# Input projection of a hybrid encoder layer: product sums kept on PSUM copies, two of four weight sums made by accumulating DMAs

## The chip, the cores and the metric

The kernel runs on one core of one Trainium2 chip. The metric is the device time of one execution in microseconds (us). Before the change it is 901.23 us, the median of three runs (899.83 to 901.51).

## The reference

One layer of an encoder is applied to 768 tokens of width 1024 (a batch of 512 and a batch of 256 tokens, side by side), in float32:

```
x    = layernorm(x_in)
proj = x @ w_in                                   # 1024 -> 3072: bg, cg, hc, q, k, v
y    = concat(rmsnorm(bg * dwconv3(cg * hc)), rmsnorm(neighbourhood_attention(q, k, v)))
x    = layernorm(ALPHA * x + y @ w_o)
u    = dwconv3(x @ w_up); gate, val = split(u)
out  = layernorm(ALPHA * x + (gelu(gate) * val) @ w_down)
```

The part that changes is `x @ w_in` without the v columns (2560 of the 3072 columns), and what reads its results.

## The kernel before

Every float32 operand of a matrix product is split into a rounded high part and the remainder (`split`, line 100: a ScalarE copy, then a subtraction on VectorE or GpSimd). A product is three matmuls of parts for each of four blocks of 128 rows, so twelve matmuls.

The input projection and the up projection multiply 2 x 2 blocks with seven products in place of eight (a Strassen-Winograd scheme). The operands on the token side are seven sums of quarters of x, kept as `AR[:, o]`; on the weight side there are seven sums of quarters of two weight blocks (g and v: q with k, cg with hc, or two bg blocks). One such set is a *pair*. The input projection has ten pairs (`SEQB`, line 342), so 70 products or 840 matmuls (line 185). Each product covers 384 token columns.

A pair before (`Pair`, line 153; `pair_steps`, line 517):
- **weights**: four quarters are loaded by SyncE's queue (SP, line 123) into a ring of six raw buffers (`NRAW`). GpSimd (POOL) makes the four weight sums as 128x512 additions (line 162). Each of the seven weight operands is then split into a ring of six `w4` buffers (ScalarE line 101, VectorE line 102).
- **products**: in the order 1, 6, 2, 5, 7, 3, 4. The products 1 and 2 share one PSUM bank, 7 and 4 share another, the other three have one each: five banks' worth a pair, taken from four `r` banks.
- **sums of products**: product 1 is copied to SBUF by ScalarE (line 531); VectorE then makes five 128x384 additions a pair out of PSUM (lines 533, 538, and three in `c22`, `c12`, `c21` of the classes `QK`, `CH`, `BB`), each of which also adds an SBUF tile.

The weights of pair n+1 are split product by product while pair n is multiplied. Between the products stand attention steps (S products, softmax, transposes, O products: `att_steps`, line 584; how many after which product is written by hand in `RATE`), and GpSimd also builds the attention's bias (line 566), issues its DMAs and adds squares (line 430). The order on SP is the program's. The other engines' order in this stage is made by a compile-time scheduler that goes by program order as priority and estimated times; each engine then runs its list in order.

Ahead of this stage come the layer norm of x, its transposes, the v projection (line 308) and the seven token operands (`x_t_sums`); the first pair's weights are split there too (`SEQA`, line 365, an order by hand, with `P7` as its last entry). After it come the output projection (lines 765, 787), the up projection (line 863, its own class `Pair` at line 838) and the down projection (line 1015).

The up projection does its pairs differently, and the change brings its way to the input projection. It loads five buffers a pair, two of which get the other quarter added by an accumulating DMA that GpSimd issues (lines 846, 847); VectorE makes the other two weight sums (lines 853, 856). The products run in the order 1, 7, 6, 2, 4, 5, 3. ScalarE copies product 1's bank to a second PSUM bank (line 917), product 6 is accumulated on the copy, that is copied again (line 924), and products 2, 4, 5 and 3 are accumulated on those three banks; product 7 is copied to SBUF (line 921) and added twice by VectorE (lines 932, 936).

Of the kernel before, what the change touches and what calls it, by code (L numbers as in the profile page):

```python
# [34 lines left out]
NRAW, NW4, NST = 6, 6, 2  # L35
NWD, NHO, NUP = 10, 10, 11
# [11 lines left out]
def encoder_kernel(ctx, tc, x, lnp, wv, wproj, wo_a, wo_c, wup, wdn, chan, rpb, mask, ident, out):  # L48
# [22 lines left out]
    def big(name):  # L71
        return ps.tile([P, 1024], F32, name=name, tag="big", bufs=2)

# [29 lines left out]

    SE = G
# [46 lines left out]
    late = {}  # L151

    class Pair:


        def __init__(self, a11, a12, a21, a22):
            self.a = {1: a11, 2: a12, 21: a21, 4: a22}
            self.t, self.o = {}, {}

        def tmp(self, i, x, y, sub, dst=None):  # L160
            t = self.t[i] = late["s"].tile([P, 512], F32, name="stmp", bufs=NST) if dst is None else dst
            (SE.tensor_sub if sub else SE.tensor_add)(t, x, y)
            return t

        def sums(self, d5=None, d6=None):
            a = self.a
            self.tmp(5, a[21], a[4], False, d5)
            self.tmp(6, self.t[5], a[1], True, d6)
            self.tmp(7, a[1], a[21], True, a[21])

        def get(self, i, tag="w4", eng=V):
            a = self.a
            if i in (5, 6) and 5 not in self.t:
                self.sums()
            if i == 3:
                self.tmp(3, a[2], self.t[6], True, a[2])
            src = a[i] if i in (1, 2, 4) else self.t[i]
            self.o[i] = wsplit(src, eng=eng) if tag == "w4" else wsplit(src, late["s"], "w4b", 2, eng)
            return self

    def prod(pi, i, q, start=True, stop=True, ks=range(4), n=slice(0, 384)):
        w = pi.o[i].rearrange("p h (k n) -> p h k n", k=4)
        for k in ks:
            for m, (g, h) in enumerate(((0, 0), (0, 1), (1, 0))):
                PE.matmul(q[:, n], w[:, g, k], ar(OPS[i])[:, h, k, n], start=start and k == 0 and m == 0,  # L185
                          stop=stop and k == 3 and m == 2, skip_group_check=i in (1, 2, 4, 7))
# [156 lines left out]
    for z in SEQB:  # L343
        p = int(z[2])
        g, v = (wproj[c * 4 + m] for c, m in {"qk": ((3, p), (4, p)), "ch": ((1, p), (2, p)), "bb": ((0, p), (0, p + 1))}[z[:2]])
        stm.add(Pair, g[:, 0:512], g[:, 512:1024], v[:, 0:512], v[:, 512:1024])
    stm.load(1)
# [9 lines left out]
    late["s"] = a1  # L357
    ORDER = (1, 6, 2, 5, 7, 3, 4)
    stm.ahead = 1
    pb = [stm.next(0)]  # L360
    stm.ahead = 2
    PW = engs("VGVGVVG")
    TA = (0, 2, 1, 3, 4, 5)
    EA = {"L": lambda i: ln_in(TA[i]), "x": lambda i: x_t(TA[i]), "v": lambda i: v_proj(TA[i], 0), "u": lambda i: v_proj(TA[i], 1), "T": x_t_sums, "P": lambda o: pb[0].get(o, eng=PW[ORDER.index(o)]), "w": lambda k: wv_prep(k, k + 1), "l": stm.load}
# [10 lines left out]
    late["s"] = a2  # L375
# [10 lines left out]
    y_d = dram.tile([2, 4, P, T], F32, name="y_d")  # L386

# [14 lines left out]
    def k_split(src, u):  # L402
        for n, m in ((slice(256 * u, 256 * u + 256), slice(0, 256)), (slice(NS + P * u, NS + P * u + P), slice(256, 384))):
            A.activation(kh[:, n], src[:, m], AF.Copy, scale=0.125)
            V.scalar_tensor_tensor(kl[:, n], src[:, m], 0.125, f(kh[:, n]), op0=OP.mult, op1=OP.subtract)
# [14 lines left out]
    def y_parts(hi, lo, src, i):  # L420
        A.activation(hi, src, AF.Copy, scale=gng[:, i:i + 1])
        V.scalar_tensor_tensor(lo, src, gng[:, i:i + 1], f(hi), op0=OP.mult, op1=OP.subtract)
# [16 lines left out]
    cy, by = {}, {}  # L439

    class QK:
# [3 lines left out]
        def c11(self, q):  # L445
            q_split(q, 0)

        def c22(self, q, t):
            z = stt()
            V.tensor_add(z, q, t)  # L450
            k_split(z, 1)

        def c12(self, q, t):
            V.tensor_add(t, q, t)
            q_split(t, 1)

        def c21(self, q, s):
            V.tensor_add(s, q, s)
            k_split(s, 0)

    class CH:
        def __init__(self, p):
            self.p = p
            self.c = a2.tile([P, T], F32, name="cp", tag="c3", bufs=2)
            self.x = a2.tile([P, T], F32, name="cc", tag="c3", bufs=2)

        def mul(self, z, u):
            for n, m, w in ((256 * u, 0, 256), (NS + P * u, 256, P)):
                V.tensor_mul(self.x[:, n:n + w], z[:, m:m + w], self.c[:, 384 * u + m:384 * u + m + w])

        def c11(self, q):
            A.copy(self.c[:, 0:384], q)

        def c22(self, q, t):
            self.z = stt()
# [232 lines left out]
    for _ in att:  # L708
        pass
# [448 lines left out]
```

## Time and profile before

| What | Value |
|---|---|
| median of three runs | 901.23 us |
| the profiled execution, whole time | 901.13 us |
| its span in the profile | 898.8 us |
| before the input projection | 0 to 61.6 us |
| input projection with attention | 61.6 to 275.0 us |
| output projection, norm, token operands | 275 to 400 us |
| up projection | 400 to 704 us |
| down projection and last norm | 704 to 898.8 us |

TensorE is busy 94% of the span, VectorE 75%, ScalarE 50%, GpSimd 27%. In the tables PE is TensorE's matmul, PEld its weight load, DVE is VectorE, ACT ScalarE, POOL GpSimd, SPq the DMA queue of SyncE. PEclk is the granted TensorE clock as a share of full speed. A row of grouped instructions gives the line, engine, operation, output<-inputs and count, then the busy time and mean duration (ns) of one, then the idle time of the engine just before them with what ended it.

### The profile page before, as it was taken

The page shows a single profiled execution, that of the slowest core. Times are in us where ns is not written, and L with a number is a line of the kernel's source. Part 1 is how long each engine was busy: PE and PEld are TensorE (multiplying, and loading weights), DVE is VectorE, ACT ScalarE, POOL GpSimd, SP SyncE. Part 2 cuts the span into 40 slices and gives each one's busy share as a digit, 9 for nine tenths or more (in the row PEclk, how much of TensorE's full clock was granted, in tenths as well). Part 3 has the DMA queues.
Part 4 walks back from the last instruction along what each step waited for, and adds up shares of the span by engine and source line. Part 5 has one row for each costly group of instructions (what it writes and reads, how often), then busy time and mean ns, then how long its engine had stood idle before and what let it go on. Part 6 is the DMA issues. An engine that isn't in the chain of part 4 may idle for free.

```text
span 898.8 us, 12782 instructions
## 1 busy us (share of the span) xinstructions
PE 840.7 (94%) x4425; PEld 777.3 (86%) x4425; DVE 671.4 (75%) x1204; ACT 447.9 (50%) x893; POOL 242.4 (27%) x269
## 2 busy tenths in 40 slices
PE   4898999989899898699999999999999999999995
PEld 3687999979898676599999999999999888888884
DVE  6988888978887588768888888888888773373356
ACT  4654465555665335456555555656566462153200
POOL 3764482554513313312222221212120100000002
PEclk9899999979999898799999999999999999999998
DMA  8565242252536610555555555565643496256012
GB/s 305 179 185 135 59 130 92 77 127 59 127 112 219 207 42 1 130 139 154 147 155 145 159 144 156 145 158 139 167 123 112 159 389 230 89 158 223 29 47 94
DMA packets 60785, 126.91 MB, mean 141 GB/s; under 512 B 9904, under 2 KB 13424, under 8 KB 60720
## 3 DMA queue, kind: packets, MB, share of 16 engines
q1 hardware_dynamic: 44448, 89.09, 29.8%
q0 software_dynamic: 15120, 33.63, 16.3%
q10 hardware_dynamic: 1152, 3.38, 1.1%
q8 instruction: 35, 0.57, 0.3%
q14 instruction: 30, 0.25, 0.1%
HBM read 105.19 MB, written 20.84 MB: 140 GB/s over the span
## 4 chain that ended last, share of the span: by engine, by line
PE 54%; DVE 4%; issue 1%; POOL 0%; ACT 0%; POOLq 0%; DVEq 0%
PE u L863 37%; PE dn L1015 17%; DVE acc L239 1%; DVE acc L236 1%; DVE st L1028 0%; DVE acc L1026 0%; DVE AR L102 0%; POOL mv L1033 0%; DVE cu L870 0%; DVE mv L1031 0%; ACT acc L793 0%; DVE mv L789 0%; DVE w L102 0%; DVE hs L102 0%; DVE mv L1032 0%
## 5 line engine op out<-in xcount | busy, mean ns | idle before, releaser
L863 PE MATMUL u<-AR,w 128*128 128x386 f32 x1848 | 332.5, 342 | 8.1 <-DVE mv L215 3.9
L863 PEld LDWEIGHTS u<-AR,w 128*128 128x128 f32 x1848 | 330.4, 190 | 9.3 <-DVE mv L215 4.2
L1015 PE MATMUL dn<-w,hs 128*128 128x512 f32 (+1 forms) x813 | 181.1, 384 | 1.0 <-DVE hs L102 1.0
L1015 PEld LDWEIGHTS dn<-w,hs 128*128 128x128 f32 x813 | 149.7, 188 | 32.1 <-DVE hs L102 1.6
L185 PE MATMUL r<-AR,w 128*128 128x384 f32 x840 | 162.2, 348 | 4.7 <-DVE st L538 2.4
L185 PEld LDWEIGHTS r<-AR,w 128*128 128x128 f32 x840 | 151.1, 195 | 5.7 <-DVE st L538 2.8
L102 DVE TENSOR_TENSOR w<-raw,w 128x512 fp32r<-128x512 f32 x120 | 99.2, 836 | 56.5 <-ACT w L101 56.1
L101 ACT CAST w<-raw 128x512 fp32r<-128x512 f32 x125 | 75.7, 617 | 122.9 <-PE dn L1015 63.7
L102 DVE TENSOR_TENSOR w<-rw,w 128x512 fp32r<-128x512 f32 x147 | 98.8, 685 | 44.0 <-ACT w L101 43.8
L101 ACT CAST w<-rw 128x512 fp32r<-128x512 f32 x147 | 90.9, 620 | 34.0 <-issue 22.4
L870 DVE SCALAR_TENSOR_TENSOR cu<-u,ch,cu 128x385 f32<-128x385 f32 (+1 forms) x88 | 52.1, 613 | 17.0 <-ACT cu L875 14.8
L847 POOL DMA_DIRECT2D rw<-in_wup x21 | 18.0, 857 | 126.6 <-DVE cu L892 105.2
L1033 POOL TENSOR_TENSOR mv<-mv,expo 128x1 f32<-128x1 f32 x6 | 5.1, 854 | 171.8 <-DVE mv L1034 171.8
L870 DVE SCALAR_TENSOR_TENSOR cu<-cu,fwn 128x385 f32<-128x385 f32 (+1 forms) x88 | 48.7, 613 | 1.5 <-ACT cu L875 1.4
L846 POOL DMA_DIRECT2D rw<-in_wup x21 | 19.1, 907 | 101.8 <-DVE w L102 69.6
L102 DVE TENSOR_TENSOR hs<-hr,hs 128x768 fp32r<-128x768 f32 x42 | 40.0, 955 | 6.6 <-ACT hs L101 5.8
L765 PE MATMUL wo<-w,AR 128*128 128x512 f32 x144 | 37.4, 419 | 2.3 <-DVE acc L771 2.3
L101 ACT CAST hs<-hr 128x768 fp32r<-128x768 f32 x42 | 34.8, 834 | 8.9 <-DMA hr<-h_d 8.0
L765 PEld LDWEIGHTS wo<-w,AR 128*128 128x128 f32 x144 | 28.6, 202 | 10.1 <-DVE acc L771 3.6
L787 PE MATMUL woc<-w,AR 128*128 128x512 f32 x144 | 36.4, 412 | 0.0
L620 ACT ACTIVATE pr<-pr,nm 128x192 f32<-128x192 f32 (+3 forms) x48 | 21.2, 442 | 26.1 <-DVE nm L617 26.1
L787 PEld LDWEIGHTS woc<-w,AR 128*128 128x128 f32 x144 | 28.2, 198 | 6.5
(184 smaller groups left out, 1100.2 us busy)
## 6 DMA issues: line engine op xcount, KB each, us to landing
rw<-in_wup SPq DMA_DIRECT2D x105, 256.0 KB, 2.8
hr<-h_d SPq DMA_DIRECT2D x42, 384.0 KB, 5.7
raw<-in_wdn SPq DMA_DIRECT2D x44, 256.0 KB, 5.7
rw<-in_wup POOLq DMA_DIRECT2D x42, 256.0 KB, 4.1
raw<-in_wproj SPq DMA_DIRECT2D x40, 256.0 KB, 3.7
h_d<-cu POOLq DMA_DIRECT2D x22, 256.0 KB, 4.0
xa_d<-xr SPq DMA_DIRECT2D x6, 512.0 KB, 4.0
v_d<-vt SPq DMA_DIRECT2D x12, 256.0 KB, 3.4
```

The lines of the kernel that those rows point to most:

```text
L101: A.copy(hi, src)
L102: eng.tensor_sub(lo, src, f(hi))
L185: PE.matmul(q[:, n], w[:, g, k], ar(OPS[i])[:, h, k, n], start=start and k == 0 and m == 0, stop=stop and k == 3 and m == 2, skip_group_ch ...
L236: V.scalar_tensor_tensor(dst[n], src[n], mv[:, 0:1], g[n], op0=OP.add, op1=OP.mult)
L620: A.activation(o, o, AF.Exp, bias=nm[:, n:n + 1], scale=-1.0, accum_out=nm[:, 4 + n:5 + n])
L765: PE.matmul(banks[t], yas(h, i, t), wt[k][:, g], start=i == 0 and m == 0, stop=i == 3 and m == 2)
L787: PE.matmul(q, ycs(h, i, t), woc[i][n][:, g], start=i == 0 and m == 0, stop=i == 3 and m == 2)
L846: G.dma_start(t[5], v[:, hi], accum_op=OP.add)
L847: G.dma_start(t[7], g[:, lo], accum_op=OP.add)
L863: PE.matmul(q, w[:, g, k], AR[:, OPS[i], h, k], start=start and n == 0, stop=stop and n == 11, skip_group_check=True)
L870: V.scalar_tensor_tensor(c[:, e, n], u[:, m], w, c[:, e, n], op0=OP.mult, op1=OP.add)
L1015: PE.matmul(qd[n, t][:, x], hs[n, c][:, i, k:k + P], wd[n, c][:, g, x], start=c == 0 and m == 0, stop=c == NC - 1 and m == 2, skip_group_c ...
```

## The change

- `Pair` takes the form of the up projection's and is shared by both. Per pair: five SP loads, two accumulating DMAs on GpSimd's queue for the sums 5 and 7, two VectorE additions for the sums 6 and 3. No GpSimd addition is left.
- The products run in the order 1, 7, 6, 2, 4, 5, 3, with product 3 of pair n after product 1 of pair n+1. Sums are kept on PSUM copies (`pstep`). ScalarE copies three times a pair, VectorE adds twice. Two extra matmuls at the first pair write two banks once (`bank_r(True)`).
- The values of the v block come out negated. The token operand 4 and others change sign; k is scaled by -0.125, the convolution's taps and two of the group norm's gains are negated (`cwn`, `gns`).
- The raw ring has eight buffers (six before). The up projection's even pairs load to it, the odd ones to a pool of nine (eleven before).
- A pair's loads are issued at the start of the pair two before it. `x_sums` has one ScalarE copy less for each pair of token tiles. `RATE` and the places of `att_prep` and `y_split` move; the splits of the attention's last two groups come after the last product. `SEQA` and `PW` stay.

```diff
-NRAW, NW4, NST = 6, 6, 2
-NWD, NHO, NUP = 10, 10, 11
+NRAW, NW4 = 8, 6
+NWD, NHO, NUP = 10, 10, 9
...
+        def __init__(self, g, v, raw):
+            lo, hi = slice(0, 512), slice(512, 1024)
+            t = {i: raw() for i in (7, 1, 5, 4, 2)}
+            for i, (w, n) in {7: (v, lo), 1: (g, lo), 5: (v, lo), 4: (v, hi), 2: (g, hi)}.items():
+                SP.dma_start(t[i], w[:, n])
+            G.dma_start(t[5], v[:, hi], accum_op=OP.add)
+            G.dma_start(t[7], g[:, lo], accum_op=OP.add)
+            self.t, self.w = t, {}
+
+        def prep(self, i, eng=V):
+            t = self.t
+            if i == 6:
+                V.tensor_add(t[1], t[1], t[5])
+                t[6] = t.pop(1)
+            elif i == 3:
+                V.tensor_add(t[6], t[6], t[2])
+                t[3] = t.pop(6)
+            self.w[i] = wsplit(t[i], eng=eng)
...
-        for z, u, v, o, e in zip(zs, (ol, oh, oh, eh), (el, ol, zs[0], zs[2]), (3, 5, 4, 6), es):
-            if o in (3, 5):
-                A.copy(z, v)
-                v = z
-            V.tensor_sub(z, u, v)
+        A.copy(zs[1], ol)
+        V.tensor_sub(zs[0], el, zs[1])
+        V.tensor_sub(zs[1], oh, zs[1])
+        V.scalar_tensor_tensor(zs[2], zs[0], -1.0, oh, op0=OP.mult, op1=OP.subtract)
+        V.scalar_tensor_tensor(zs[3], zs[2], -1.0, eh, op0=OP.mult, op1=OP.subtract)
...
-    ORDER = (1, 6, 2, 5, 7, 3, 4)
+    ORDER = (1, 7, 6, 2, 4, 5, 3)
...
+    def pstep(n, i):
+        z, pi = SEQB[n], pb[n]
+        if i == 1:
+            K[n] = {"qk": QK, "ch": CH, "bb": BB}[z[:2]](int(z[2]))
+            R[n, 1], R[n, 2] = bank_r(), bank_r(True)
+            pi.prod(1, R[n, 1], True, False, 384)
+            A.copy(R[n, 2], R[n, 1])
+        elif i == 7:
+            R[n, 4] = bank_r()
+            pi.prod(7, R[n, 4], True, True, 384)
+            M7[n] = stt()
+            A.copy(M7[n], R[n, 4])
+        elif i == 6:
+            R[n, 3] = bank_r(True)
+            pi.prod(6, R[n, 2], False, False, 384)
+            A.copy(R[n, 3], R[n, 2])
+        elif i == 2:
+            pi.prod(2, R[n, 1], False, True, 384)
+            K[n].g(R[n, 1], 0)
+        elif i in (4, 5):
+            u = i - 4
+            q = R[n, 2 + u]
+            pi.prod(i, q, False, not u, 384)
+            v = K[n].dst(u) if z[:2] == "bb" else stt()
+            V.tensor_add(v, q, M7[n])
+            K[n].v(v, u)
+        else:
+            pi.prod(3, R[n, 3], False, True, 384)
+            K[n].g(R[n, 3], 1)
...
-    YK, AK = (2, 4, 5), 6
+    YK, AK = (2, 4), 5
...
+        load_pair()
+        steps = [(n, 1)] + [(n - 1, 3)] * (n > 0) + [(n, i) for i in (7, 6, 2, 4, 5)]
+        nxt = iter(ORDER)
+        for k, (m, i) in enumerate(steps):
+            pstep(m, i)
+            if n + 1 < len(SEQB):
+                for o in [next(nxt, 0)] + ([next(nxt, 0)] if k == 5 and n == 0 else []):
+                    if o:
+                        pb[n + 1].prep(o)
...
+    pstep(len(SEQB) - 1, 3)
+    y_split(ya_l[2], 2)
     for _ in att:
         pass
+    y_split(ya_l[3], 3)
```

## Rows read from the trace of the kernel before

**Rows 1.** Busy time of each engine in three stages, with granted clock.

```profile
core 0: us, PE busy (x) PEld busy (x) DVE busy (x) ACT busy (x) POOL busy (x), PEclk, DMA share, GB/s
0.00:61.60 61.60, 45.27 (x192) 34.74 (x193) 52.00 (x76) 36.93 (x66) 33.73 (x30) 0.94 0.66 221
61.60:275.00 213.40, 200.40 (x1211) 196.50 (x1210) 179.48 (x407) 119.72 (x337) 101.65 (x120) 0.96 0.39 106
400.00:704.00 304.00, 304.00 (x1721) 303.95 (x1720) 244.75 (x408) 180.10 (x310) 62.89 (x79) 1.00 0.54 146
```

**Rows 2.** What TensorE waited for, 61 to 276 us: total, times, longest.

```profile
PE PT L632 <- DVE pr L623: 3.6, 3, 2.2
PE r L185 <- DVE st L538: 2.4, 1, 2.4
PE S L599 <- DVE kl L405: 1.9, 2, 1.6
PE O L665 <- DVE pt L646: 1.5, 2, 1.3
PE r L185 <- ACT st L531: 1.3, 1, 1.3
PE S L599 <- ACT kh L404: 1.1, 1, 1.1
PE r L185 <- DVE st L450: 1.0, 1, 1.0
```

**Rows 3.** TensorE's timeline, one unbroken run of products; then the stretch 192 to 195 us.

```profile
122.11 19.18 PE L185 MATMUL r<-AR,w 128*128 128x384 f32 x108
...
192.00:195.00 3.00, 2.25 (x11) 2.24 (x12) 2.96 (x8) 0.58 (x1) 0.57 (x1) 0.50 0.78 185
```

**Rows 4.** Timelines of POOL and DVE around 190 us: start, us.

```profile
188.70 1.29 POOL L162 TENSOR_TENSOR stmp<-raw 128x512 f32<-128x512 f32 x1
...
190.14 2.55 DVE L623 TENSOR_SCALAR pr<-pr,nm 128x192 f32<-128x192 f32 x2
```

**Rows 5.** Groups of instructions, whole span: weight sums and sums of products.

```profile
L162 POOL TENSOR_TENSOR stmp<-stmp,raw 128x512 f32<-128x512 f32 x10 | 14.3, 1433 | 0.7
...
L162 POOL TENSOR_TENSOR raw<-raw,stmp 128x512 f32<-128x512 f32 x10 | 13.8, 1379 | 27.5 <-DVE w L102 11.7 <-issue 11.0 <-DMA raw<-in_wproj 4.6
...
L533 DVE TENSOR_TENSOR st<-r,st 128x384 f32<-128x384 f32 x10 | 5.4, 541 | 0.4 <-PE r L185 0.4
```

**Rows 6.** Groups of the up projection: weight sums, accumulating DMA, copies.

```profile
L846 POOL DMA_DIRECT2D rw<-in_wup x21 | 19.1, 907 | 101.8 <-DVE w L102 69.6 <-DMA rw<-in_wup 18.7 <-ACT w L101 8.4
...
L853 DVE TENSOR_TENSOR rw<-rw 128x512 f32<-128x512 f32 x21 | 14.5, 691 | 0.7
...
L917 ACT COPY u<-u 128x386 f32<-128x386 f32 x22 | 10.2, 466 | 30.7 <-PE u L863 30.7
```

**Rows 7.** Weight splits on DVE: input projection (61 to 276 us), up projection (whole span).

```profile
L102 DVE TENSOR_TENSOR w<-raw,w 128x512 fp32r<-128x512 f32 x52 | 50.2, 967 | 8.5 <-ACT w L101 8.2
...
L102 DVE TENSOR_TENSOR w<-rw,w 128x512 fp32r<-128x512 f32 x147 | 98.8, 685 | 44.0 <-ACT w L101 43.8
```

**Rows 8.** Chain that ended last: one seed matmul of the up projection.

```profile
400.21 0.18 PE u L909
```

**Rows 9.** DMA issues: KB each, median us from issue to landing.

```profile
rw<-in_wup POOLq DMA_DIRECT2D x42, 256.0 KB, 4.1
...
raw<-in_wproj SPq DMA_DIRECT2D x40, 256.0 KB, 3.7
...
vw<-v_d POOLq DMA_DIRECT2D x8, 384.0 KB, 11.4
```

**Rows 10.** Timelines of SP, ACT and PE ahead of the input projection.

```profile
11.94 0.33 SPq L335 DMA_DIRECT2D raw<-in_wv  x1
...
18.49 0.62 ACT L101 CAST w<-raw 128x512 fp32r<-128x512 f32 x1 [0.33 <-DMA raw<-in_wv]
...
19.16 2.56 PE L308 MATMUL vp<-w,AR 128*128 128x512 f32 x9 [1.59 <-ACT w L101]
```

**Rows 11.** ACT's timeline at the first products: the last split of the first pair.

```profile
64.12 0.62 ACT L101 CAST w<-raw 128x512 fp32r<-128x512 f32 x1 [1.47 <-PE r L185]
```

More of the change, by code (lines that the diff above doesn't have):

```diff
@@ L149, in plain, with raw_ring @@
         return [wsplit(r) for r in raw]
-    late = {}
+    def raw_ring():
+        return ring.tile([P, 512], F32, name="raw", bufs=NRAW)
+    TERMS = ((0, 0), (0, 1), (1, 0))
     class Pair:
[L156 to L186, printed above, removed]
+        def __init__(self, g, v, raw):
[6 more added lines that the diff above has]
+            self.t, self.w = t, {}
@@ new lines, in prep, with prod @@
+        def prep(self, i, eng=V):
[7 more added lines that the diff above has]
+            self.w[i] = wsplit(t[i], eng=eng)
+        def prod(self, i, q, start, stop, n=HT):
+            w = self.w.pop(i).rearrange("p h (k n) -> p h k n", k=4)
+            for m, (k, (g, h)) in enumerate((k, z) for k in range(4) for z in TERMS):
+                PE.matmul(q, w[:, g, k], AR[:, OPS[i], h, k, 0:n], start=start and m == 0, stop=stop and m == 11, skip_group_check=True)
@@ L342, in encoder_kernel, with load_pair @@
     SEQB = ("qk0", "ch0", "bb0", "qk1", "ch1", "qk2", "ch2", "qk3", "ch3", "bb2")
[L343 to L347, printed above, removed]
+    pb = []
+    def load_pair():
+        if len(pb) < len(SEQB):
+            z = SEQB[len(pb)]
+            p = int(z[2])
+            g, v = (wproj[c * 4 + m] for c, m in {"qk": ((3, p), (4, p)), "ch": ((1, p), (2, p)), "bb": ((0, p), (0, p + 1))}[z[:2]])
+            pb.append(Pair(g, v, raw_ring))
+    load_pair()
     NWV = 2
@@ L495, in __init__, with g, dst, v @@
                 by[p + i] = a2.tile([P, T], F32, name="b", bufs=2)
-        def c11(self, q):
-            A.copy(by[self.p][:, 0:384], q)
-        def c22(self, q, t):
-            V.tensor_add(by[self.p + 1][:, 384:768], q, t)
-        def c12(self, q, t):
-            V.tensor_add(by[self.p][:, 384:768], q, t)
-        def c21(self, q, s):
-            V.tensor_add(by[self.p + 1][:, 0:384], q, s)
-            gate(self.p)
-            gate(self.p + 1)
+        def g(self, q, u):
+            A.copy(by[self.p][:, 384 * u:384 * u + 384], q)
+            if u:
+                for p in (self.p, self.p + 1):
+                    full.add(p)
+                    gate(p)
+        def dst(self, u):
+            return by[self.p + 1][:, 384 * u:384 * u + 384]
+        def v(self, z, u):
+            pass
     def gate(p):
-        if p in cy and p in by:
+        if p in cy and p in full:
             y = cy.pop(p)
@@ L515, in gate, with bank_r @@
             G.dma_start(y_d[0, p], y)
[L517 to L547 removed]
+    def bank_r(seed=False):
+        q = ps.tile([P, 512], F32, name="r", bufs=4)[:, 0:384]
+        if seed and len(R) < 4:
+            PE.matmul(q, AR[:, 0, 0, 0, 0:P], AR[:, 0, 0, 0, 0:384], start=True, stop=True, skip_group_check=True)
+        return q
+    R, M7, K = {}, {}, {}
+    def pstep(n, i):
[27 more added lines that the diff above has]
+            K[n].g(R[n, 3], 1)
     bias, vwin = {}, {}
@@ L680, in att_steps @@
         else:
-            y_split(ya, 3)
+            ya_l[3] = ya
     def att_in(k):
@@ L895, in gated, with load_up @@
         G.dma_start(z[:, :, 256:384], g[:, :, Z0 + 1:Z1])
-    pairs, R, M7, seeded = {}, {}, {}, []
-    def early_raw():
-        return ring.tile([P, 512], F32, name="raw", bufs=NRAW)
+    pairs, R, M7 = {}, {}, {}
+    def load_up(c):
+        pairs[c] = Pair(wup[c], wup[NC + c], up_raw if c % 2 else raw_ring)
     def up_raw():
@@ L967, in encoder_kernel @@
     seq = seq[1:]
-    ready = {(0, i) for i in ORDU}
+    ready = {(0, i) for i in ORDER}
     def prepare(c, i):
@@ L1052, in encoder_kernel @@
             if i == 7 and c + 1 < NC:
-                pairs[c + 1] = Pair(c + 1, up_raw)
+                load_up(c + 1)
             step(c, i)
```

135 lines of the change are left out of this document (34 added, 101 removed).

## The prediction

> **What bounds the kernel now.** I read first the busy times by stage [rows 1]. In the up projection TensorE is busy for all of 304.0 us at a granted clock of 1.00. In the input projection, 213.4 us long, it is busy for 200.4 us: 13.0 us idle. Its mean clock there is 0.96, which costs at most (1 - 0.96) x 213.4 = 8.5 us more. So a change that keeps the number of matmuls can win at most 13.0 + 8.5 = 21.5 us there. VectorE is busy for 179.5 of the 213.4 us (84%), GpSimd for 101.7 us.
>
> Then the list of waits says what ends TensorE's idle time [rows 2]: seven kinds, 12.8 us together. Three of them, 4.7 us (lines 538, 531, 450), are sums or copies of products that were late, so that a PSUM bank was not free. The other 8.1 us are attention steps (lines 623, 405, 646, 404) whose input was late. All but two (2.4 us) are VectorE's. A product's pitch comes from the unbroken run of 108 matmuls [rows 3]: the next entry starts 19.0 us later, so 0.176 us a matmul and 2.11 us for the twelve of a product.
>
> The timelines around 190 us show how a wait comes about [rows 4]. Line 623 handled two tiles in 2.55 us while GpSimd ran its weight sums beside it, and TensorE's longest wait for it was 2.2 us [rows 2]. Behind it TensorE ran at the lower of its two levels: 0.50 (1.2 GHz) from 192 to 195 us [rows 3]. An idle gap thus costs up to (13.0 + 8.5) / 13.0 = 1.65 times its length.
>
> **The change, part by part.**
>
> Matmuls: 840 stay 840. Two seeds are added, each 0.18 us by the seed of the up projection [rows 8]: +0.4 us.
>
> GpSimd: forty weight sums go, in four groups of 13.8 to 14.3 us [rows 5], about 56 us. Twenty accumulating DMAs come, at most 0.907 us each to issue [rows 6]: 18 us. Net -38 us on an engine that isn't the bound; its worth is what it does to VectorE.
>
> VectorE: fifty additions out of PSUM become twenty, 30 x 0.541 [rows 5] = -16.2 us. Twenty weight sums come: 0.691 us each as in the up projection [rows 6], up to 0.967 us if they stretch as the splits do here [rows 7], so +13.8 to +19.3 us. Up to here that is about nothing. But the 52 weight splits of raw tiles take 967 ns here and 685 ns in the up projection [rows 7], in all 52 x 0.282 = 14.7 us. The difference I put down to GpSimd's work beside them, busy 48% of this stage and 21% of that one [rows 1]. The weight sums are about half of GpSimd's work here, so about -7 us. VectorE then falls from 179 to some 172 us.
>
> ScalarE: three copies a pair in place of one, 20 x 0.466 [rows 6] = +9.3 us on 119.7 us [rows 1]. It is not the bound, but two of the three copies stand in TensorE's way, which is the price further down.
>
> DMA: three transfers a pair more, 30 x 256 KB = 7.9 MB on 213 us, 37 GB/s beside 106 GB/s [rows 1]. They are hidden: loads go out at the start of the pair two before their use, so a pair's 213.4 / 10 = 21 us and more lie ahead. On SP's queue a load waits for a free raw buffer, and the next loads wait behind it; eight buffers for five a pair leave the last two (4 and 2) to wait for the previous pair's splits of 7 and 3, still some 8 us ahead of use against 3.7 us of landing [rows 9]. On GpSimd's queue each accumulating DMA waits for its load; behind it stand bias, bias loads and attention loads, which GpSimd's idle half covers. From issue to landing it took 4.1 us in the up projection; the slowest of this queue's loads took 11.4 us [rows 9], which also fits into 21 us.
>
> Ahead of the stage: two loads of the v weights no longer wait for a raw buffer. Such a load went out at 11.94 us; a split at 18.49 us still waited 0.33 us for one, and TensorE 1.59 us for ScalarE [rows 10]. Bounds 0 and -1.6 us; I take -1.0, since the load was late but the split queue of that engine stays. VectorE is busy there for 52.0 of 61.6 us [rows 1]; two weight sums more are made up by GpSimd's four less.
>
> Start of the stage: the split of `P7` is last in its list. It waited until 64.12 us for the first product to free a `w4` buffer [rows 11]. Product 7 was the fifth then, and is the second now. Its operand would be there at 64.12 + 0.62 + about 1.3 us for GpSimd's subtraction. Covered by products 6 and 2 if the scheduler puts those ahead (then only ScalarE's copy, 0.47 us, shows), uncovered one product, 2.1 us. I take +0.7 us.
>
> What goes of the 21.5 us: bounds 0 (all waits come from attention) and 21.5 (all go). The 4.7 us of late sums and copies hang on operations that go or move, and the 3.6 us of line 623 on GpSimd's sums beside it: 8.3 of 12.8 us. But VectorE stays over 80% busy, GpSimd keeps its bias work, and the late k and O tiles stay. I take half: -10.7 us.
>
> What comes: two couplings a pair have only one product, 2.1 us, as cover. Product 4 accumulates on a bank that ScalarE copies after product 6, with product 2 between; product 3 accumulates on a bank that VectorE reads after product 5, with the next pair's product 1 between. In the up projection the second has two products as cover. Where ScalarE stands in an Exp that waits for VectorE, the copy behind it is late, and product 4 with it. Bounds: 0, as in the up projection, and 20 x 1.3 x 1.65 = 43 us, if each of the twenty costs as much as the copy of line 531 did once [rows 2], with the clock. The near row is that of this stage, where three waits of this kind stood against 70 products; I take two: 2 x 1.3 x 1.65 = +4.3 us.
>
> Sum: 0.4 - 1.0 + 0.7 - 10.7 + 4.3 = -6.3 us. The profiled execution took 901.1 us (span 898.8 us), as the median, 901.2 us: 894.8 us. The later stages I cost at nothing: their matmuls stay, the up projection has 17 raw buffers for two pairs, and the last two `y_split`s have 36 matmuls of the output projection ahead of their use.
>
> One rule of the Trainium skill looks at the room in another way ("Perfetto Trace Analysis", Identifying the Most-Contended Engine): a busy share of the matmuls says little, that of the weight loads more. The weight loads are busy for 196.5 us [rows 1], so the idle room would be 16.9 instead of 13.0 us, half of the losses 12.7 instead of 10.7 us, and the result 892.8 us. No row here says that the 3.9 us between the two could be used.
>
> **The rivals.**
> - *All losses go*, as in the up projection, whose 304 us are full with VectorE 80% busy. For it: the same order and copies. Against it: no attention there. Time: 901.1 - 21.5 + 0.1 = 879.7 us. Chance 0.15.
> - *No change*: attention sets the waits, and its chain (line 623 and the k and O tiles, 8.1 of 12.8 us) isn't touched; then what the sums win, the copies take. Time 900 to 903 us. Chance 0.14.
> - *Slower*: the couplings of one product decide. ScalarE's copy stands behind Exps and casts, so product 4 starts late, TensorE idles, and the clock falls. Each costs 1.3 x 1.65 = 2.1 us, and the gains of 10.7 are eaten from the fifth of twenty on; at nine it is 901.1 - 10.9 + 19 = 909 us. For it: ScalarE's load grows and its order is fixed ahead by estimates. Against it: it is busy for only 56% [rows 1]. Chance 0.22.
> - *Accumulating DMAs late*: VectorE's operations hold up what GpSimd issues, the splits of 5 and 7 are late in every pair. At 3 us for nine pairs 901.1 + 27 = 928 us; it would need a landing of over 21 us where the slowest row of that queue has 11.4 [rows 9]. Chance 0.02. The Trainium skill has such a rule ("SBUF — State Buffer", Who interferes with whom: VectorE's two-port modes keep GpSimd from writing descriptors); the 42 such DMAs of the up projection landed in 4.1 us beside a VectorE busy 80%.
>
> **How the numbers follow.** The forecast has the chance 0.47 and its own range 887 to 899. A measurement of this kernel can tell about 0.2% (1.8 us) from no change, so faster means below 899.4 and slower above 903.0. Faster: 0.47 + 0.15 + 0.04 of the no-change case = 0.66. Same: 0.09. Slower: 0.22 + 0.02 + 0.01 of the no-change case = 0.25. The range leaves out the lower half of the all-go case (0.08) and the upper half of the slower one with the late DMAs (0.13): 882 to 906.
>
> **What would show it.** Right: GpSimd without additions of raw tiles; splits on VectorE in this stage below 900 ns; the stage some 205 us long; the waits for line 623 shorter; a few new waits of products for ScalarE's second copy or VectorE's addition. Wrong: product waits for that copy in most pairs (slower), waits for S, O and transposes as long as before (no change), or a mean clock of 1.00 in the whole stage (all go). A gap in front of the second product at 64 us that is longer than 2 us, or a later stage that moves by over 2 us, would also stand against the sum.

## The result, and the profile after

The changed kernel takes 889.53 us, the median of four runs (882.95 to 889.81), beside 901.07 us for the kernel before on the same chip: a ratio of 0.9864 [0.9833, 0.9895], so faster by 11.5 us. The forecast was 894.8 us. The profiled execution took 889.39 us (span 887.6 us).

The places where TensorE's stages begin, from the timelines of its first products, say where the time went. It isn't where the prediction put it:

| stretch | before, us | after, us | difference |
|---|---|---|---|
| up to the first product of the input projection | 61.8 | 57.9 | -4.0 |
| input projection | 213.1 | 213.3 | +0.2 |
| output projection, norm, token operands | 89.1 | 84.3 | -4.8 |
| up projection | 339.7 | 339.0 | -0.7 |
| down projection, last norm | 195.1 | 193.1 | -2.0 |

The table compares one profile of each kernel. In it the stage that the change was costed for gained nothing (in a second profile of the kernel after, further down, 3 us), though its engines did what was forecast. Busy times by stage of the kernel after, with the columns of [rows 1]:

```profile
0.00:57.70 57.70, 43.01 (x193) 33.01 (x193) 48.74 (x81) 34.62 (x62) 26.38 (x27) 1.00 0.78 253
57.70:271.20 213.50, 201.18 (x1212) 193.91 (x1211) 154.21 (x392) 129.38 (x359) 76.58 (x105) 0.97 0.57 140
```

VectorE fell from 179.5 to 154.2 us, GpSimd from 101.7 to 76.6 us; the DMA engines' share rose from 0.39 to 0.57. The groups of VectorE (weight splits of this stage, beside [rows 7]) and of GpSimd (its accumulating DMAs):

```profile
L99 DVE TENSOR_TENSOR w<-raw,w 128x512 fp32r<-128x512 f32 x68 | 50.8, 749 | 26.0 <-ACT w L98 25.6
```

```profile
L160 POOL DMA_DIRECT2D raw<-in_wproj x9 | 9.1, 1011 | 14.3 <-DMA raw<-in_wproj 12.5 <-DVE w L99 1.0 <-DVE nm L613 0.8
L161 POOL DMA_DIRECT2D raw<-in_wproj x9 | 8.4, 931 | 45.6 <-DVE kl L403 13.3 <-DVE pt L638 12.3 <-DMA raw<-in_wproj 10.5
```

A split of a raw tile takes 749 ns in place of 967. The last column is to be noted for later: GpSimd stands 14.3 + 45.6 us ahead of these DMAs, 23.0 us of it put down to the loads that they add to, and none of TensorE's waits listed next names them. What TensorE waited for in this stage (total, times, longest), beside [rows 2]:

```profile
PE PT L624 <- DVE pr L615: 6.0, 1, 6.0
PE r L177 <- ACT w L98: 1.3, 1, 1.3
PE O L657 <- DVE pt L638: 1.2, 2, 0.6
PE r L177 <- DVE st L535: 1.2, 1, 1.2
PE r L177 <- POOL w L99: 1.0, 1, 1.0
PE r L177 <- DVE b L535: 0.7, 1, 0.7
```

Before, seven kinds of short waits; now most of them are gone, and one wait of 6.0 us and two at the stage's start (1.3 and 1.0 us) have come. The wait of 6.0 us for the transposes' input, in the timeline of ACT, DVE and PE at 196 us, then ACT's and POOL's timelines ahead of it:

```profile
196.31 0.26 ACT L652 COPY ya<-O 64x128 f32<-64x128 f32 x1 [4.92 <-DMA y_d<-ya]
...
197.10 0.17 DVE L613 RECIPROCAL nm<-nm 128x2 f32<-128x2 f32 x1 [5.00 <-ACT pr L612]
...
197.80 1.08 PE L624 MATMUL PT<-idt,pr 128*128 128x128 f32 x4 [6.00 <-DVE pr L615]
```

```profile
177.45 1.09 ACT L663 COPY ya<-O 64x64 f32<-64x64 f32 x8
...
181.16 2.03 POOL L570 DMA_DIRECT2D vw<-v_d  x3
183.17 0.61 POOL L671 DMA_DIRECT2D y_d<-ya  x1
```

Read it backwards. TensorE waits for VectorE, VectorE for ScalarE's Exp, and ScalarE stands at the copy into `ya` (one buffer) until the store of the previous pair of heads has read it. That store went out on GpSimd's queue at 183.2 us, 4.6 us after the last copy into `ya` had ended (178.5 us), behind three loads of `vw`; it landed 13.1 us later. The same wait stood in a second profile of the unchanged kernel after (6.7 us), so it isn't chance. In the kernel before, nothing waited for the same store. Its rows on ACT's timeline, then on POOL's:

```profile
184.09 1.09 ACT L671 COPY ya<-O 64x64 f32<-64x64 f32 x8
...
200.30 0.53 ACT L660 COPY ya<-O 64x128 f32<-64x128 f32 x2
```

```profile
185.47 0.60 POOL L679 DMA_DIRECT2D y_d<-ya  x1 [0.88 <-ACT ya L671]
```

There it went out 0.3 us after `ya` was full (185.2 us), landed 12.3 us later and so 2.5 us ahead of the next copy. So 7.4 us were lost between the two kernels: 4.3 us because GpSimd issues the store later, 2.3 us because the next copy into `ya` comes sooner (12.8 in place of 15.1 us after `ya` is full), and only 0.8 us because the transfer itself takes longer. The store's row among the DMA issues (KB each, median us to landing, of all three stores), and the windows around, with the columns of [rows 1]:

```profile
y_d<-ya POOLq DMA_DIRECT2D x3, 384.0 KB, 14.3
```

```profile
189.00:192.00 3.00, 2.80 (x21) 2.47 (x20) 2.72 (x9) 2.00 (x5) 0.00 (x0) 1.00 1.01 244
195.00:198.00 3.00, 0.20 (x1) 0.21 (x2) 0.86 (x4) 1.02 (x4) 0.00 (x0) 0.65 0.62 133
198.00:201.00 3.00, 3.00 (x12) 3.00 (x12) 1.78 (x8) 1.57 (x5) 0.00 (x0) 0.50 0.06 12
```

Ahead of the gap the DMA engines are full (1.01); behind it TensorE runs at 0.50, its lower level of 1.2 GHz, for three microseconds more. The start of the stage, on TensorE's timeline:

```profile
61.43 0.62 PE L177 MATMUL r<-AR,w 128*128 128x384 f32 x2 [1.32 <-ACT w L98]
...
63.41 2.93 PE L177 MATMUL r<-AR,w 128*128 128x384 f32 x8 [1.01 <-POOL w L99]
```

Product 7, now the second, waits for both halves of the split `P7`, the last of the list.

### The profile page after: what moved, and what is told of

It is laid out like the page before. It is cut to its first block, busy times and chain, and to the rows that moved or that the text cites. A ratio compares the mean times of both kernels' runs of the same rounds, so it can differ in the third digit from the quotient of the medians.

```text
span 887.6 us, 12748 instructions
## 1 busy us (share of the span) xinstructions
PE 836.3 (94%) x4427; PEld 771.2 (87%) x4427; DVE 640.8 (72%) x1197; ACT 455.3 (51%) x912; POOL 207.1 (23%) x249
## 4 chain that ended last, share of the span: by engine, by line
PE 55%; DVE 3%; issue 1%; ACT 1%; POOL 0%; POOLq 0%; DVEq 0%
PE u L177 37%; PE dn L987 18%; DVE acc L230 1%; DVE acc L227 0%; DVE st L1000 0%; DVE AR L99 0%; DVE acc L998 0%; ACT w L98 0%; POOL mv L1005 0%; DVE cu L842 0%; DVE mv L1003 0%; ACT acc L796 0%; DVE mv L792 0%; DVE hs L99 0%; POOLq L1126 0%
## 5 line engine op out<-in xcount | busy, mean ns | idle before, releaser
L99 DVE TENSOR_TENSOR w<-raw,w 128x512 fp32r<-128x512 f32 x208 | 147.1, 717 | 90.9 <-ACT w L98 90.4
L98 ACT CAST w<-raw 128x512 fp32r<-128x512 f32 x215 | 131.2, 619 | 149.7 <-PE dn L987 63.9
L99 DVE TENSOR_TENSOR w<-rw,w 128x512 fp32r<-128x512 f32 x77 | 51.8, 685 | 24.3 <-ACT w L98 24.2
L842 DVE SCALAR_TENSOR_TENSOR cu<-u,ch,cu 128x385 f32<-128x385 f32 (+1 forms) x88 | 52.2, 613 | 16.4 <-ACT cu L847 14.3
L98 ACT CAST w<-rw 128x512 fp32r<-128x512 f32 x77 | 47.6, 620 | 18.1 <-issue 11.8
L866 POOL DMA_DIRECT2D h_d<-cu x22 | 15.6, 710 | 168.9 <-DVE cu L864 148.7
L300 PE MATMUL vp<-w,AR 128*128 128x512 f32 x108 | 29.1, 415 | 2.9 <-DVE AR L99 1.1
L998 DVE TENSOR_TENSOR acc<-dn,acc 128x512 f32<-128x512 f32 (+1 forms) x13 | 8.3, 647 | 27.9 <-PE dn L987 27.8
```

The lines of the kernel that those rows point to most:

```text
L98: A.copy(hi, src)
L99: eng.tensor_sub(lo, src, f(hi))
L300: PE.matmul(q, x_part(t, c)[:, h, k], wvo[4 * c + k][:, g], start=c + m + k == 0, stop=c == 1 and m == 2 and k == 3)
L842: V.scalar_tensor_tensor(c[:, e, n], u[:, m], w, c[:, e, n], op0=OP.mult, op1=OP.add)
L866: G.dma_start(z[:, :, 0:256], g[:, :, 0:Z0])
L998: V.tensor_add(o, qd[n, t][:, x:x + w], o)
```

## The experiments

Two theories stood against each other. *Mine after the result*: the stage would have gained, but the late store of `ya` and the late `P7` took it back. *The rival*: VectorE or the one-product couplings set the length of the stage anyway, so mending these two waits only moves them. Each ratio is to the kernel before on the same chip.

**The changed kernel again**, as the bar for the runs beside it (no edit).

> The changed kernel, nothing edited, for a comparison on one chip with the runs beside it. Both theories: its ratio to the kernel before stays at 0.986, within 0.003.

888.98 us, 0.9875 [0.9839, 0.9912]. In its profile the stage takes 209.9 us: two executions of one kernel differ by 3.4 us in this stage, so smaller differences between single profiles are not read below.

**The store on another queue.**

```diff
-            G.dma_start(y_d[1, p], ya)
+            A.dma_start(y_d[1, p], ya)
```

> The changed kernel, with one edit: the store of the attention result ya goes out on ScalarE's DMA queue in place of GpSimd's. In the changed kernel TensorE stood still for 6.0 us at 191.8 us, behind a ScalarE copy into ya that waited 4.9 us for the store of the ya before, issued 13 us earlier between two loads of vw on the same queue. Theory A (the store is held up by its queue): it lands within 6 us, the 6.0 us wait goes, and with it the low clock behind it: 882 to 884 us, every run near 883. Theory B (the 16 DMA engines are full at that time, whatever the queue): the store still takes over 10 us and the time stays at 888 to 890 us.

882.52 us, 0.9823 [0.979, 0.9855]. Not every run is near 883: two of the six took 887 us, the profiled one among them (887.44 us), and its stage is hardly shorter (211.3 us). So the gain stands in the median and not in this trace. The landing of the three stores, the second of them on ACT's timeline with the loads of `vw` on POOL's, and the longest wait of TensorE in the stage:

```profile
DMA to landing us min/median/max: 2.6/7.4/11.1
```

```profile
178.78 0.33 ACTq L671 DMA_DIRECT2D y_d<-ya  x1
...
181.35 2.66 POOL L570 DMA_DIRECT2D vw<-v_d  x4
```

```profile
PE O L648 <- DMA vw<-v_d: 2.6, 1, 2.6
```

The wait of 6.0 us is gone, and the next late thing shows: the loads of `vw` themselves. The median of the landings, 7.4 us in place of 14.3, hides how it went. The second store, the one that TensorE had waited for, goes out as soon as `ya` is full, 2.6 us ahead of the loads of `vw`, and lands after 2.6 us. The first and the third go out while loads of `vw` are under way and land after 7.4 and 11.1 us, though no load is on their queue. So theory A holds for the store that mattered, because ScalarE's list doesn't hold it back; for the third, theory B is nearer.

**`P7` split earlier.**

```diff
-... P5 T2 u5 P4 P3 P7"
+... P5 T2 u5 P7 P4 P3"
```

> The changed kernel with the first pair's weight splits in the order 7, 4, 3 at the end in place of 4, 3, 7, so that product 7's operand no longer waits for the first product to free a buffer. In the changed kernel TensorE stood still there for 1.3 us (a cast) and 1.0 us (GpSimd's subtraction) and ran the 63 to 66 us at half clock. Theory gap (these 2.3 us and the low clock are on the path): 3 to 4 us less than the changed kernel beside it, both waits gone. Theory slack (VectorE is late with the token operands there, and products wait for those next): less than 1 us.

885.37 us, 0.983 [0.9793, 0.9868], 3.6 us less than the changed kernel beside it, and both waits at the start are gone. So the gap cost some 3.6 us, more than its 2.3 us of idle time: in the changed kernel the clock was 0.50 behind it (63 to 66 us). The size is rough, as the two kernels' runs overlap (884.18 to 887.99 and 886.06 to 891.66 us).

**Both edits.**

> The changed kernel with both edits, the ya store on ScalarE's queue and product 7's weights split earlier. If both gaps are on the path and independent, their gains add: 9 to 11 us less than the changed kernel beside it, so a ratio to the kernel before of 0.974 to 0.977. If the stage is bound by the transfers that follow the store, only the first 3 us show: ratio 0.979 or more.

880.16 us, 0.977 [0.973, 0.981], 8.8 us below the changed kernel beside it, and the best kernel of this study. Its stage, TensorE's longest waits in it, and the landing of the stores:

```profile
57.70:262.40 204.70, 197.80 (x1211) 190.25 (x1210) 153.11 (x391) 129.29 (x359) 72.19 (x102) 0.99 0.61 146
```

```profile
PE O L648 <- DMA vw<-v_d: 2.9, 2, 2.8
PE PT L624 <- DVE pr L615: 0.9, 1, 0.9
```

```profile
DMA to landing us min/median/max: 2.5/2.7/12.9
```

The last row is the landing of the three stores; the two short ones went out ahead of the loads of `vw`, the third (12.9 us) while they were under way. The gains add up within the noise of the runs. The stage is 8.4 us shorter than before and 8.6 us shorter than in the first profile of the kernel after (5.2 us against its second). The rival falls: with VectorE's work and the couplings untouched, 204.7 us is possible.

**Half of the `vw` loads on ScalarE's queue too**, in the kernel with both edits.

```diff
-            G.dma_start(f(vw[0:4 * w])...
+            (G, A)[j % 2].dma_start(f(vw[0:4 * w])...
```

> The changed kernel with its two mends (880 us), and two of the four loads of vw per pair of heads issued on ScalarE's queue instead of POOL's. In the mended kernel the four loads, issued together at 174.7 us, land after 13.6 and 11.4 us in the median, and the one wait for them that is left costs 2.8 us of TensorE with the clock at 0.75 in the six microseconds behind it, some 4 us in all. If POOL's queue is what makes them late, as it was for the store of ya: landings of 6 to 9 us, the wait gone, 875 to 878 us. If it is the DMA engines (their share is 0.90 to 1.12 in 176 to 188 us): landings as before, 879 to 882 us. If six more DMA issues on ScalarE delay the copies that the splits wait for: slower by 1 to 4 us.

890.17 us, 0.9911 [0.9886, 0.9936], ten microseconds worse than without it. The DMA issues, then a wait of ScalarE:

```profile
vw<-v_d POOLq DMA_DIRECT2D x4, 384.0 KB, 13.5
...
vw<-v_d POOLq DMA_DIRECT2D x4, 288.0 KB, 13.4
y_d<-ya ACTq DMA_DIRECT2D x3, 384.0 KB, 16.8
```

```profile
ACT w L98 <- DMA vw<-v_d: 3.9, 1, 3.9
```

The loads left on GpSimd's queue land no earlier (13.5 and 13.4 us), as the theory of full DMA engines says; for those on ScalarE's queue the profile has no landing. It has one for a single store of `ya`, 16.8 us: that store went out 1.7 us behind a load of `vw` on ScalarE's queue, and no wait followed from it. ScalarE's 3.9 us stand at the start of the stage (63.4 to 67.2 us), where it issues the first of these loads. How ten microseconds come out of this is not worked out wait by wait.

**The weight sums back on GpSimd**, input projection only.

```diff
-            G.dma_start(t[5], v[:, hi], accum_op=OP.add)
-            G.dma_start(t[7], g[:, lo], accum_op=OP.add)
+            G.tensor_add(t[5], t[5], t[4])
+            G.tensor_add(t[7], t[7], t[1])
...
-                V.tensor_add(t[1], t[1], t[5])
+                G.tensor_add(t[1], t[1], t[5])
...
-                V.tensor_add(t[6], t[6], t[2])
+                G.tensor_add(t[6], t[6], t[2])
```

> The changed kernel with all four weight sums of the input projection on GpSimd as 128x512 additions, as before, and no accumulating DMA there; the products stay on PSUM copies. Theory contention: first product two to four us later, weight splits in the stage back above 850 ns on average, waits of TensorE for attention steps longer by some us: 894 us or more. Theory products (the gain comes from the order and the copies of the products, the ring and the moved steps): within 2 us of 889.5. Against both works that 20 loads and the accumulation are gone: the 6.0 us wait for the store at 191.8 us may shrink.

914.01 us, 1.0162 [1.0128, 1.0196]: the PSUM copies and the new order without the new sums are slower than the kernel before. The splits of this stage take 842 ns on average (749 in the kernel after, above 850 forecast), and TensorE's waits for the softmax, the q tiles and O come to 10.5 us. The same layer norm step ahead of the stage, DVE's and POOL's timeline, in this kernel and then DVE's in the kernel after:

```profile
33.64 1.29 POOL L99 TENSOR_TENSOR w<-raw,w 128x512 fp32r<-128x512 f32 x1
...
33.83 3.33 DVE L232 SCALAR_TENSOR_TENSOR xr<-xr,mv,gb 128x512 f32<-128x512 f32 x2
34.88 1.72 POOL L172 TENSOR_TENSOR raw<-raw 128x512 f32<-128x512 f32 x1
```

```profile
34.10 1.40 DVE L227 SCALAR_TENSOR_TENSOR xr<-xr,mv,gb 128x512 f32<-128x512 f32 x2
```

Beside a split's subtraction and a weight sum on GpSimd VectorE's pair of operations takes 3.33 us, without them 1.40. The first product starts at 60.0 us here and at 57.9 after: some two of the four microseconds won ahead of the stage.

**Two sums on VectorE in place of the accumulating DMAs.**

```diff
-            G.dma_start(t[5], v[:, hi], accum_op=OP.add)
-            G.dma_start(t[7], g[:, lo], accum_op=OP.add)
...
+                    V.tensor_add(t[a], t[a], t[b])
```

Tile 4 is added to 5 ahead of operand 6, tile 1 to 7 ahead of operand 7.

> The changed kernel with the sums 5 and 7 of the input projection as VectorE additions on buffers that are loaded anyway; no accumulating DMA there, so 5.2 MB less to load, and twenty additions of 0.69 us more on VectorE. Theory transfers (the stage is held up by transfers that bunch when an attention group changes): the 6.0 us wait at 191.8 us goes or falls under 3 us; 4 us or more less than the changed kernel beside it. Theory VectorE (its load decides, and taking sums off it or off GpSimd is the gain): 14 us more on VectorE bring new waits for attention steps, and the time rises by 3 us or more.

907.08 us, 1.008 [1.005, 1.0109], 18.1 us above the changed kernel beside it. VectorE's waits, and the stage:

```profile
DVE raw L173 <- DMA raw<-in_wproj: 26.7, 9, 9.4
```

```profile
57.80:291.60 233.80, 205.49 (x1212) 197.26 (x1210) 167.03 (x413) 130.39 (x362) 59.89 (x87) 0.93 0.40 107
```

VectorE has 13 us more to do, and it stands 26.7 us in line for loads. The wait for the softmax that cost 6.0 us is down to 0.8 us, as the theory of transfers forecast, but TensorE now waits 9.2 and 7.2 us for the q tiles. More work and more waiting are mixed here; the next run parts them.

The loads that VectorE stands for are late because they go out late. SP's and DVE's timelines at the longest wait:

```profile
196.63 0.33 SPq L159 DMA_DIRECT2D raw<-in_wproj  x1
...
208.68 0.69 DVE L173 TENSOR_TENSOR raw<-raw 128x512 f32<-128x512 f32 x1 [9.38 <-DMA raw<-in_wproj]
```

SP sent this load when a split on VectorE had ended and freed a raw buffer (196.6 us), and it landed 12.0 us later. In eight of the nine waits SP had held the load until an operation of VectorE had ended; the nine landed 2.5 to 12.0 us after they went out. So the ring of eight raw buffers has a part in the 26.7 us. A deeper ring with the sums on VectorE was not tried.

**The same 18 additions on VectorE, without new loads to wait for.**

```diff
+            if i == 7 and self is not pb[0]:
+                V.tensor_add(t[1], t[1], t[7])
+                V.tensor_sub(t[1], t[1], t[7])
```

> In nine of the ten pairs VectorE adds the seventh raw tile to the first and takes it off again, which changes only the last bits of the weights: 18 more VectorE operations of 128x512 at 0.69 us (12.5 us), as many as the two sums that the accumulating DMAs do, on tiles that are there already, so that VectorE waits for no load that it did not wait for before. Theory that moving those two sums to VectorE cost 18 us because VectorE then stands in line for the loads: this kernel loses little of it, 889 to 896 us, and its stage of the input projection takes 213 to 220 us. Rival, that VectorE has no room for 12.5 us more in this stage whatever it waits for: 903 to 909 us, a stage of 227 to 234 us. In either case the accumulating DMAs stay, so their transfers are the same.

891.08 us, 0.9894 [0.9835, 0.9954]; the stage:

```profile
58.00:273.10 215.10, 201.04 (x1212) 192.46 (x1211) 163.83 (x410) 129.75 (x359) 76.28 (x105) 0.98 0.57 139
```

The edit does more than its text says. The up projection uses the same class, so its 22 pairs get the two operations as well: 62 operations in all, 18 of them in this stage. Even so, nearly the same work in the stage (163.8 us on VectorE in place of 154.2) costs about two microseconds. So what an accumulating DMA is worth here is not the 0.7 us of VectorE that it saves: its wait for a load stands in GpSimd's list, where the 23.0 us above show in none of TensorE's waits, and not in VectorE's, where splits and softmax stand behind it.

**VectorE's sums with the two mends.** The two edits above, on the kernel with the sums on VectorE.

> The kernel with all four weight sums on VectorE and no accumulating DMA, with the two mends that brought the changed kernel to 880 us (the store of ya on ScalarE's queue, product 7's weights prepared earlier). If standing in line for loads is what it suffers from, the mends do not reach it: 902 to 907 us, with waits of VectorE for loads of 20 us or more left in the stage. If instead its loss was made of the same two things (the store behind the loads of vw, the start of the stage), it falls with them, to 880 to 890 us, and the accumulating DMAs are worth little.

898.78 us, 0.9974 [0.9935, 1.0012]. Neither forecast held: the mends took off about as much as they did from the changed kernel (8.3 us, between two chips whose kernel before differs by 0.3 us), while VectorE's waits stayed:

```profile
DVE raw L173 <- DMA raw<-in_wproj: 20.2, 7, 8.3
```

The two losses are separate and add. The landing of the three stores of `ya`, all on ScalarE's queue, where no load stood, and all sent while loads of `vw` were under way:

```profile
DMA to landing us min/median/max: 9.3/11.1/12.8
```

So a queue of its own does not make the store quick; going out ahead of the loads does.

**Six raw buffers in place of eight**, in the changed kernel (`NRAW, NW4 = 6, 6`).

> The changed kernel with six raw buffers in place of eight. The projection's first product starts at 57.9 us in the changed kernel and at 61.8 us before. Theory ring (two loads of v weights no longer wait for a buffer): with six the first product starts at 61 us or later, and the time rises by 3 us or more. Theory contention (GpSimd's weight sums of the first pair are gone from beside VectorE's layer norm): it starts at 58 us as with eight, and the time changes by less than 2 us, unless the later pairs' loads, with only one spare buffer, come late and add waits of products in the stage.

913.66 us, 1.0151 [1.0115, 1.0187]. The first product starts at 57.97 us, as with eight: the eight buffers have no part in the gain ahead of the stage, against my step. They matter in the stage. VectorE's weight sums there, then TensorE's longest wait:

```profile
L167 DVE TENSOR_TENSOR raw<-raw 128x512 f32<-128x512 f32 x9 | 6.2, 692 | 23.9 <-DMA raw<-in_wproj 23.9
```

```profile
PE PT L624 <- DVE pr L615: 19.1, 5, 8.2
```

Again VectorE stands in line, 23.9 us, and the attention behind it waits. Here it stands for the accumulating DMAs, which land 5.8 to 14.0 us after GpSimd sends them. So they keep VectorE out of the line only as long as there are buffers enough.

**One ScalarE copy less in `x_sums`, in the kernel before.**

```diff
-            if o in (3, 5):
-                A.copy(z, v)
-                v = z
-            V.tensor_sub(z, u, v)
+        A.copy(zs[1], ol)
+        V.tensor_sub(zs[0], zs[1], el)
+        V.tensor_sub(zs[1], oh, zs[1])
...
```

> The kernel before, with the change's one copy less in the token sums (same operands, same signs as before). Theory copy (ScalarE's three copies of 0.58 us stood in the way ahead of the stage): first product about 60 us in place of 61.8, time 1 to 2 us down. Theory contention or ring: first product at 61 to 62 us, time within 1 us of 901.

901.84 us, 1.0037 [1.001, 1.0064]: nothing won by this part. Its profile shows 66.0 us up to the first product and 83.7 us for the output projection and what follows, where the kernel before had 61.8 and 89.1: the borders between these stretches move by 4 to 5 us with a change that leaves the total alone. Taken together, the two stretches are steadier: 150.9 and 149.7 us in the profiles of the kernel before and of this one, 139.4 to 143.9 us in the twelve profiles of the kernel after and its variants, also where the stage between them takes 20 us longer. So 6 to 11 us of the gain stand there. The up projection (339.0 to 341.0 us) and the stretch behind it (193.2 to 195.4 us) are within the spread of these profiles the same. Which part of the change shortens the two stretches no run shows; the ring and the one copy don't.

**Product 3 one product later.** It changes part of the computation: the first attention scores behind a pair of q and k are made before that pair's last part has been added.

```diff
-        steps = [(n, 1)] + [(n - 1, 3)] * (n > 0) + [(n, i) for i in (7, 6, 2, 4, 5)]
+        steps = [(n, 1), (n, 7)] + [(n - 1, 3)] * (n > 0) + [(n, i) for i in (6, 2, 4, 5)]
```

> Product 3 of the pair before is put one product later, behind product 7, so that the copy of product 6's sum has two products of cover in every pair instead of one in two of them. If the couplings with one product of cover cost what the waits for line 535 show (1.2 + 0.7 us), and those waits go: 1 to 3 us less than the changed kernel beside it, 886 to 889 us. If the cover was enough and those waits are something else: the same, within 1 us. If holding the psum tile for one product longer delays the next pair: slower by 1 to 4 us.

891.55 us, 0.9915 [0.9885, 0.9946], not faster. TensorE's waits in the stage:

```profile
PE S L591 <- ACT qh L397: 9.5, 3, 8.9
...
PE r L177 <- DVE st L535: 1.0, 1, 1.0
```

The wait for line 535 doesn't go: 1.0 us of it stands before the eighth product again, which is now product 7 of the second pair. And in this profile attention waits 8.9 us once. But it is the profile of the slowest of the ten executions (899.91 us, the others 888.87 to 893.68 us), so the long wait may not stand in the others. The run doesn't isolate the couplings' price; it shows only that more cover for product 3 brought nothing.

## Why the prediction was right, and where its working was not

The forecast was faster, by 6.3 us; it was 11.5 us, inside the range. That it came out so near is partly luck: by stretch the sum gave -1.0 us ahead of the stage, -5.3 in it and 0 behind it, and the first profiles show -4.0, +0.2 (-3.1 in the second profile of the kernel after) and -7.5.

- **What goes of the 21.5 us (-10.7).** The step held once the two new waits were mended: then the stage takes 204.7 us, 8.4 us less than before. The waits for lines 623, 405, 646 and 404 of [rows 2], 8.1 us together, are down to 1.9 us there (0.9 for the softmax, the others 0.2 to 0.4), and VectorE is stretched less by GpSimd, which was the reason given. The run with the sums back on GpSimd agrees: such waits were 10.5 us there.
- **"They are hidden" (DMA) failed.** I counted whether the accumulating loads come in time; they do, 4.8 us from issue to landing. I put at nothing what else stands in GpSimd's list, and overlooked the store of `ya` there: the slowest row of that queue was this store, 12.3 us, not the 11.4 us that I named. It ran into the one buffer of `ya`. Of the 7.4 us that it lost against the kernel before, 4.3 us are its later issue, 2.3 us the earlier next copy and 0.8 us the slower transfer, so the 7.9 MB more are the least of it. Price: 5.2 us beside the mended start (885.37 against 880.16).
- **Start of the stage (+0.7; bound 2.1) was mis-sized.** The place was right, the uncovered case came true, 2.3 us idle, and with the clock behind it some 3.6 us. I had multiplied the other waits by 1.65 for the clock, and not this one; 2.1 x 1.65 = 3.5 us.
- **Couplings (two, +4.3).** Two waits for line 535 stand in the list, 1.2 and 0.7 us, each shorter than 1.3 us, and the rival of nine or more did not come about. The two rows together, with 1.65, would be 3.1 us. That there are two is luck: the first stands before the eighth product, product 3 of the first pair, as forecast; the second before the last product of all, which follows product 5 with no product between, a coupling that I hadn't counted. None is a wait of product 4 for ScalarE's copy. (In the rival *Slower* the gains add up to 10.6 us, not 10.9; nothing hangs on it.)
- **VectorE (172 us) was mis-sized**, in the safe direction: 154.2 us. I gave the splits half of their stretching back, 7 us. All 70 of the stage, those of the temporary sums included, took 932 ns on average before (50.2 us in [rows 7] and 15.0 us below) and 749 ns after; on 68 that is 12.4 us. And I left out the softmax: its scaling of the larger tiles fell from 635 to 347 ns, and with the 192-column tiles from 17.7 to 9.4 us. The splits of temporary sums before, then the scaling before and after:

```profile
L102 DVE TENSOR_TENSOR w<-stmp,w 128x512 fp32r<-128x512 f32 x18 | 15.0, 831 | 2.5 <-ACT w L101 2.4
```

```profile
L623 DVE TENSOR_SCALAR pr<-pr,nm 128x256 f32<-128x256 f32 x16 | 9.5, 635 | 0.2
```

```profile
L615 DVE TENSOR_SCALAR pr<-pr,nm 128x256 f32<-128x256 f32 x16 | 4.9, 347 | 0.1
```

  ScalarE's +9.3 us measured +9.7.
- **Ahead of the stage (-1.0) was mis-sized and had the wrong cause.** It was -4.0 us, and the ring has no part in it. About two come with GpSimd's additions leaving (60.0 against 57.9 us). The granted clock of this stretch was 0.94 before and 1.00 after, and 1.00 as well with the additions back; why it rose, and with it the rest, is open.
- **The later stages (0) failed**: -7.5 us, of which 4.8 us at the output projection. Windows there of the kernel before, then of the kernel after:

```profile
296.00:300.00 4.00, 1.83 (x4) 1.02 (x5) 1.50 (x2) 3.86 (x9) 1.55 (x2) 0.73 0.94 357
300.00:305.00 5.00, 5.00 (x13) 3.90 (x14) 4.23 (x8) 0.95 (x2) 0.53 (x1) 0.54 0.07 24
```

```profile
292.00:296.00 4.00, 2.42 (x8) 1.53 (x8) 0.82 (x2) 0.00 (x0) 2.61 (x2) 0.86 1.06 336
296.00:300.00 4.00, 4.00 (x14) 3.21 (x13) 3.58 (x6) 3.45 (x7) 2.58 (x3) 0.71 0.28 54
```

  TensorE was idle for 2.2 of the first four microseconds and at 0.54 behind them. The kernel after has the same gap four microseconds earlier, 1.6 us of it, and 0.71 behind it, so this gap is only a little shorter. Over the whole stretch TensorE's waits fell from 8.2 to 5.8 us and the granted clock rose from 0.92 to 0.96; in the kernel before with one copy less it was 1.00. As that edit moved this border by 5 us as well, one profile of each doesn't show that the change did this; the sum of the two stretches around the stage, further up, does show a gain, whose cause is open.
- **Accumulating DMAs late (0.02)** stayed away. The page's rule behind it, in the Trainium skill "SBUF — State Buffer", Who interferes with whom, found no case here: the twenty landed after 4.8 us in the median. The weight-load rule ("Perfetto Trace Analysis") gave 892.8 us, nearer to 889.5 by the total; the stage that it spoke of does not bear it out, as it shrank by 3 us at most.

## What to carry to other kernels

An operation that waits for a load costs little in a list where nothing critical stands behind it, and much in the list of a busy engine: two of the sums cost 18 us more on VectorE than as accumulating DMAs, though the additions alone are worth two at most. How much of that a deeper ring of buffers would give back was not tried. When a change adds work to a list, look not only at the new transfers but at every store in it whose buffer an engine will want back: how long after its tile is full does it go out, and which loads are under way then? When a change moves an operand's use forward, move its preparation too, and price the gap with the clock behind it.

## What the runs showed of the hardware that I had not expected

- A store of 384 KB landed after 2.5 to 2.7 us (three stores) when it went out ahead of the loads of `vw`. Sent while they were under way, it landed after 7.4 to 12.9 us on ScalarE's queue with no load on it (six stores), and after 12.8 to 15.3 us on GpSimd's queue together with them (nine stores of the kernel after in two profiles and of the one with `P7` earlier). The Trainium skill has a rule that bears on it ("DMA: Bandwidth & Descriptors", Queues, rings and completion order): each DMA engine takes turns between the queues that have work for it. By that a store on a queue of its own gets its turn while loads run; the landings agree in that it was mostly sooner than behind them, but it was still far from quick.
- Two layer norm operations of VectorE took 3.33 us beside a subtraction and an addition of GpSimd and 1.40 us without, a factor of 2.4, where I had reckoned with the factor 1.4 of the splits (967 to 685 ns).
